# A decoder trunk on one core: the first FFN products formed as Strassen's seven block products, weights split in parts of 1024 columns

## Chip, core and metric

One core of a Trainium2 chip runs the whole program. The metric is device time in microseconds (us), the median of the runs. TensorE (PE) multiplies, VectorE (DVE), ScalarE (ACT) and GpSimd (POOL) work beside it, and SyncE (SP) starts the transfers. Instructions of one engine run in the order in which they stand; a tile scheduler fixes that order when the program is built, by priorities and by which buffers are free.

## What is computed

512 tokens of 1024 features pass through two layers. Each layer has a mixer and an FFN, both behind an RMS norm and added to the residual. The FFN is what changes most:

```python
def swiglu(x, w1, w3, w2):
    return (jax.nn.silu(x @ w1) * (x @ w3)) @ w2
```

`w1` and `w3` are 1024 x 2816, `w2` is 2816 x 1024. The mixer of layer 0 has six input projections to 512 columns, a linear recurrence and a retention; the one of layer 1 has five projections and attention in three branches.

## The kernel before

The residual `h` lies with features on the partitions, as 8 tiles of 128 x 512 tokens. Every float32 operand of a large product is split into a high part rounded to float32r and a low remainder, and the product is the sum of three passes, high-high, low-high and high-low (`mm3`, lines 123 to 125). For the normed residual `put_hg` does this (lines 136, 137); for weights `fetch` does it: a unit of 128 x 2048 is loaded into a buffer `wr` (pool of 2), and in four pieces of 512 columns ACT rounds `whi` (line 98) and DVE takes `wlo = wr - whi` (line 99; pools of 3 each). `unit` runs two units ahead of the products, at a priority a little above its place.

```python
 529  s = self.g2([P, S], name="s")
 530  V.tensor_tensor(s, pu, rb, op=ALU.mult)
 531  A.activation(s, s, AF.Silu)
 532  v = self.g2([P, S], name="v")
 533  V.tensor_tensor(v, pv, rb, op=ALU.mult)
 534  Q.tensor_tensor(v, v, s, op=ALU.mult)
 535  gh[j], gl[j] = ghq[:, j - q0, :], glq[:, j - q0, :]
 536  A.copy(gh[j], v)
 537  V.tensor_tensor(gl[j], v, gh[j].bitcast(F32), op=ALU.subtract)
```

An FFN (`ffn`, quoted from a hidden tile's end) works in two halves of 11 hidden tiles. For each hidden tile it forms two products, `ps_u` with w1 and `ps_v` with w3, each of 8 feature tiles times 3 passes = 24 matmuls with the weights stationary and 512 tokens moving. DVE scales both by the token's RMS factor (lines 530, 533), ACT applies silu (531), POOL multiplies (534), ACT and DVE split the result into `gh`, `gl` (536, 537). Then w2 is applied: 8 products `ps` of 11 x 3 matmuls, each added to `h` by DVE (552). In the second half of the last FFN the last two feature tiles run by halves of 256 tokens, and `final` scales and stores. While the residual is formed ACT squares each tile (148) and POOL sums the squares in `acc` (150); `stat_r` turns them into RMS factors after the first 24 matmuls of the FFN (matmul 160, DVE 163, POOL power 165).

A projection (`project` in layer 0, `proj` in layer 1) takes the tokens stationary: for each of 4 token tiles 8 x 3 matmuls into one PSUM bank `ps_t`, so that the first token tile already needs both units of the weights. PSUM has four banks in `psA`, two each in `psB` and `psC`. Transposes on PE (`ps_tr`) use `psC`.

Of the kernel before, what the change touches and what calls it, by code (L numbers as in the profile page):

```python
# [7 lines left out]

# [13 lines left out]
P = 128  # L22
# [19 lines left out]
QUADS = ((0, 4), (4, 4), (8, 3))  # L42


class Trunk:
    def __init__(self, ctx, tc, a, out, dbg=None, upto=99):
# [13 lines left out]
        self.units = []  # L60
        self.ready = []
# [24 lines left out]
    def plan(self, name, idx, n):  # L86
        self.units.append((self.a[name][idx], n))

    def blank(self):
        """buffers for the next unit: raw, its source, hi, lo"""  # L90
        src, n = self.units.pop(0)
        w = self.wr.tile([P, 2048], F32, tag="wr", name="wr")
        hi = self.wh.tile([P, 2048], F32R, tag="wh", name="whi")
        lo = self.wl.tile([P, 2048], F32R, tag="wl", name="wlo")
        return w[:, 0:n], src, hi, lo

    def split(self, w, hi, lo, c):
        self.nc.scalar.copy(hi[:, c], w[:, c])  # L98
        self.nc.vector.tensor_tensor(lo[:, c], w[:, c], hi[:, c].bitcast(F32), op=ALU.subtract)  # L99

    def fetch(self):
        with self.tc.high_priority(offset=10):
            w, src, hi, lo = self.blank()
            self.nc.sync.dma_start(w, src)
            n, k = w.shape[1], 4
            for i in range(k):
                self.split(w, hi, lo, slice(i * n // k, (i + 1) * n // k))
        self.ready.append((hi, lo))

    def prefetch(self, n):  # L110
        while self.units and len(self.ready) < n:
            self.fetch()

    def unit(self, ahead=2):
        self.prefetch(1 + ahead)
        return self.ready.pop(0)

    def mm3(self, ps, terms, first=True, last=True):
        """ps = sum over terms of (lhs_hi + lhs_lo)^T (rhs_hi + rhs_lo)"""
        mm = self.nc.tensor.matmul  # L120
# [12 lines left out]
    def put_hg(self, hg, k, h, gcol):  # L133
# [3 lines left out]
        nc.vector.scalar_tensor_tensor(lo, h, gcol, hi.bitcast(F32), op0=ALU.mult, op1=ALU.subtract)  # L137

# [14 lines left out]
    def stat_r(self, tiles=range(NT), last=None):  # L153
        """1/rms of token tiles as [P, len(tiles)]"""
# [13 lines left out]
    def stat_bc(self, r):  # L168
        """1/rms broadcast over partitions, [P, tokens] in PSUM"""
# [12 lines left out]
    def setup(self):  # L182
# [5 lines left out]
        # keeps the tensor engine busy until the first operands are there, so that its clock is up by then  # L188
# [5 lines left out]
        # loads the activation table  # L194
# [38 lines left out]
    def softplus(self):  # L233
        """4 and -8 times softplus(-lam), [P, 4]"""
# [27 lines left out]
    def layer0(self):  # L262
        nc, a = self.nc, self.a
        V, A, Q, T = nc.vector, nc.scalar, nc.gpsimd, nc.tensor
        for u in range(12):
            self.plan("w0t", u, 2048)
# [7 lines left out]
        wx = [self.blank() for _ in range(2)]  # L274
        self.stat_start()
        for k in range(KD):
            x = xin[k // 4][:, k % 4, :]
            w, src, hi, lo = wx[k // 4]
            c = slice((k % 4) * S, (k % 4 + 1) * S)
            nc.sync.dma_start(w[:, c], src[:, c])  # L280
# [43 lines left out]
        def units():  # L324
            return [tuple(x.rearrange("p (k c) -> p k c", k=4) for x in self.unit()) for _ in range(2)]
# [836 lines left out]
```

## Time and profile before

| | |
|---|---|
| median of 3 runs (1300.49 to 1301.39) | 1300.63 us |
| span of the profiled execution | 1299.8 us |
| PE busy (matmul) | 1272.5 us, 98%, 6067 instructions |
| PE weight loads | 1049.6 us, 81% |
| DVE busy | 708.7 us, 55% |
| ACT busy | 531.7 us, 41% |
| POOL busy | 300.0 us, 23% |
| granted TensorE clock, mean | 0.994 of full speed |

The profiled execution's own time is taken as its span and the 0.8 us that the median lies above it, 1300.6 us. The program runs through these stretches (us from the span's start): loads and layer 0's mixer to 231, its FFN 231 to 594, layer 1's mixer to 928, its FFN to 1292, the end of the stores. A busy PE does not mean a matmul at its peak: neighbouring matmuls overlap in the records, so the price of one is the distance between two starts.

### The profile page before, as it was taken

How to read it: one execution, taken by the hardware profiler on the slowest of the kernel's cores; microseconds unless marked ns; L12 is line 12 of the kernel's file. 1: busy time of each engine (PE TensorE's matmuls, PEld its weight loads, DVE VectorE, ACT ScalarE, POOL GpSimd, SP SyncE). 2: the span in 40 equal slices, each digit the busy share in tenths (PEclk: the TensorE clock that was granted, in tenths of full speed). 3: DMA queues.
4: the chain of work that ended last, by engine and by line, in shares of the span. 5: the costliest groups of instructions: out<-in, count | busy, mean ns of one | idle time of the engine just before them, and what ended most of it. 6: DMA issues, size and time to landing. Idle time of an engine off the chain costs nothing.

```text
span 1299.8 us, 15778 instructions
## 1 busy us (share of the span) xinstructions
PE 1272.5 (98%) x6067; PEld 1049.6 (81%) x6067; DVE 708.7 (55%) x1215; ACT 531.7 (41%) x1121; POOL 300.0 (23%) x304
## 2 busy tenths in 40 slices
PE   8979999999999999999999999999999999999997
PEld 6668888888888888888788877877888888888887
DVE  7994446555423554443345789987345443455433
ACT  6432253433222333334445578996333222233230
POOL 3351421211100111122000467672211100011111
PEclk9999999999999999999999999999999999999999
DMA  6213052222233222252110000024222223322221
GB/s 235 93 65 130 1 185 78 94 97 87 69 120 130 97 97 67 96 198 84 65 65 33 1 1 1 33 66 162 97 98 98 67 89 120 111 95 88 74 71 65
DMA packets 24042, 114.58 MB, mean 88 GB/s; under 512 B 2688, under 2 KB 5008, under 8 KB 14624
## 3 DMA queue, kind: packets, MB, share of 16 engines
q1 hardware_dynamic: 23776, 112.45, 24.9%
q8 instruction: 48, 0.79, 0.2%
q0 software_dynamic: 192, 1.13, 0.2%
q14 instruction: 26, 0.21, 0.0%
HBM read 109.38 MB, written 4.19 MB: 87 GB/s over the span
## 4 chain that ended last, share of the span: by engine, by line
PE 87%; DVE 7%; issue 2%; POOL 2%; ACT 1%; DMA 0%; POOLq 0%; SPq 0%; DVEq 0%; ACTq 0%
PE ps_v L123 6%; PE ps_u L125 6%; PE ps_v L125 6%; PE ps_u L123 6%; PE ps_u L124 6%; PE ps_v L124 6%; PE ps L125 6%; PE ps L123 6%; PE ps L124 6%; PE ps_t L123 4%; PE ps_t L124 4%; PE ps_t L125 4%; PE ps_tr L929 2%; PE ps_s L904 1%; PE ps_p L124 1%
## 5 line engine op out<-in xcount | busy, mean ns | idle before, releaser
L98 ACT CAST whi<-wr 128x512 fp32r<-128x512 f32 (+1 forms) x416 | 212.5, 576 | 394.2 <-PE ps_v L124 162.4
L99 DVE TENSOR_TENSOR wlo<-wr,whi 128x512 fp32r<-128x512 f32 (+1 forms) x416 | 294.4, 763 | 44.3 <-ACT whi L98 44.1
L534 POOL TENSOR_TENSOR v<-v,s 128x512 f32<-128x512 f32 x44 | 67.5, 1535 | 523.2 <-DVE v L533 506.9
L123 PE MATMUL ps<-gh,whi 128*128 128x512 f32 (+1 forms) x374 | 141.0, 377 | 0.0
L124 PE MATMUL ps<-gl,whi 128*128 128x512 f32 (+1 forms) x374 | 140.8, 376 | 0.0
L125 PE MATMUL ps<-gh,wlo 128*128 128x512 f32 (+1 forms) x374 | 140.8, 376 | 0.0
L533 DVE TENSOR_TENSOR v<-ps_v,rbc 128x512 f32<-128x512 f32 x44 | 30.4, 691 | 198.0 <-PE ps_v L125 198.0
L123 PE MATMUL ps_v<-hgh,whi 128*128 128x512 f32 x352 | 137.1, 390 | 0.0
L123 PE MATMUL ps_u<-hgh,whi 128*128 128x512 f32 x352 | 137.1, 390 | 0.0
L125 PE MATMUL ps_u<-hgh,wlo 128*128 128x512 f32 x352 | 137.0, 389 | 0.0
L124 PE MATMUL ps_u<-hgl,whi 128*128 128x512 f32 x352 | 136.9, 389 | 0.0
L124 PE MATMUL ps_v<-hgl,whi 128*128 128x512 f32 x352 | 136.9, 389 | 0.0
L125 PE MATMUL ps_v<-hgh,wlo 128*128 128x512 f32 x352 | 136.9, 389 | 0.0
L124 PE MATMUL ps_t<-wlo,hgh 128*128 128x512 f32 x288 | 113.3, 393 | 6.7 <-DVE wlo L99 6.7
L123 PE MATMUL ps_t<-whi,hgh 128*128 128x512 f32 x288 | 116.0, 403 | 0.0
L125 PE MATMUL ps_t<-whi,hgl 128*128 128x512 f32 x288 | 113.6, 394 | 0.0
L552 DVE TENSOR_TENSOR h<-ps,h 128x512 f32<-128x512 f32 x30 | 20.8, 692 | 135.4 <-PE ps L125 135.4
L924 POOL TENSOR_TENSOR prob<-prob,rs 128x384 f32<-128x384 f32 (+3 forms) x128 | 88.5, 726 | 1.9
L150 POOL TENSOR_TENSOR acc<-acc,sq 128x512 f32<-128x512 f32 (+1 forms) x35 | 48.9, 1398 | 172.1 <-ACT sq L148 171.9
L124 PEld LDWEIGHTS ps<-gl,whi 128*128 128x128 f32 x374 | 70.4, 188 | 13.0
L123 PEld LDWEIGHTS ps<-gh,whi 128*128 128x128 f32 x374 | 70.4, 188 | 12.8
L125 PEld LDWEIGHTS ps<-gh,wlo 128*128 128x128 f32 x374 | 70.4, 188 | 12.8
(282 smaller groups left out, 2291.7 us busy)
## 6 DMA issues: line engine op xcount, KB each, us to landing
wr<-wff SPq DMA_DIRECT2D x44, 1024.0 KB, 4.8
wr<-w SPq DMA_DIRECT2D x32, 704.0 KB, 4.0
wr<-w0t SPq DMA_DIRECT2D x10, 1024.0 KB, 4.8
wr<-w1t SPq DMA_DIRECT2D x10, 1024.0 KB, 4.9
wr<-w0o SPq DMA_DIRECT2D x4, 1024.0 KB, 4.8
wr<-w1o SPq DMA_DIRECT2D x4, 1024.0 KB, 4.9
wr<-w0t SPq DMA_DIRECT2D x8, 256.0 KB, 5.4
xin<-xT SPq DMA_DIRECT2D x8, 256.0 KB, 5.4
```

Of the source, the lines that this page charges most:

```text
L98: self.nc.scalar.copy(hi[:, c], w[:, c])
L99: self.nc.vector.tensor_tensor(lo[:, c], w[:, c], hi[:, c].bitcast(F32), op=ALU.subtract)
L123: mm(ps, ah, bh, start=(first and k == 0), stop=False)
L124: mm(ps, ah, bl, start=False, stop=False)
L125: mm(ps, al, bh, start=False, stop=(last and k == n - 1))
L150: nc.gpsimd.tensor_tensor(self.acc[:, c], self.acc[:, c], sq, op=ALU.add)
L533: V.tensor_tensor(v, pv, rb, op=ALU.mult)
L534: Q.tensor_tensor(v, v, s, op=ALU.mult)
L552: V.tensor_tensor(hm, ps, hm, op=ALU.add)
L904: T.matmul(u.ps, q, u.kh, start=True, stop=False)
L924: Q.tensor_tensor(x, x, u.rs[:, r, b:b + 1].broadcast_to([P, u.nk]), op=ALU.mult)
L929: T.transpose(u.pt[:, r * P:(r + 1) * P], u.p[:, r, b, j * P:(j + 1) * P], self.ident)
```

## The change

The hidden units of an FFN are now taken in three phases of two blocks: blocks of 512 units (`wff`), the last of 256 (`wfg`). For a block the product [v | u] = x [w3 | w1] is a product of 2 x 2 blocks: x by token halves of 256 and by even and odd feature tiles, the weights by even and odd feature tiles and by w3 and w1. `strassen` forms it from seven products, of two token tiles times four feature tiles times three passes = 24 matmuls each, with the tokens stationary and the weights' 512 columns moving. The combinations of x (`sg`: A11, A12, A22, S1 to S4) are formed once for a layer by `put_sg`; the combinations of the weights are formed on POOL in the raw buffers (line 160) before each part is split. The results are token-major; after silu and the multiplication (736) `turn` transposes them on PE (721) for w2, which is applied phase by phase.

Weights are split in parts of 1024 columns, ACT in two casts (136) and DVE in one subtraction (137). `whi` and `wlo` have 4 buffers of 1024 columns, `wr` 4 of 2048; the split runs three parts ahead. Projections go through `stream_t`: pairs of feature tiles outside, the four token tiles inside, in four banks at once. The attention's `probs` now takes its buffers from `wr` alone. The core of the diff:

```diff
-        self.wr = e(tc.tile_pool(name="wr", bufs=2))
-        self.wh = e(tc.tile_pool(name="wh", bufs=3))
-        self.wl = e(tc.tile_pool(name="wl", bufs=3))
+        self.wr = e(tc.tile_pool(name="wr", bufs=BUFS_W))
+        self.wh = e(tc.tile_pool(name="wh", bufs=BUFS_W))
+        self.wl = e(tc.tile_pool(name="wl", bufs=BUFS_W))
...
+    def split(self, x):
+        n = x.shape[1]
+        hi, lo = (t[:, 0:n] for t in self.pair())
+        k = 2 if n > 512 else 1
+        for i in range(k):
+            c = slice(i * n // k, (i + 1) * n // k)
+            self.nc.scalar.copy(hi[:, c], x[:, c])
+        self.nc.vector.tensor_tensor(lo, x, hi.bitcast(F32), op=ALU.subtract)
+        return hi, lo
...
+        def parts():
+            b11, b21 = self.take(), self.take()
+            h = [slice(c, min(c + 1024, n)) for c in range(0, n, 1024)]
+            sub = lambda o, x, y: Q.tensor_tensor(o, x, y, op=ALU.subtract)
+            b12 = None
+            for c in h:
+                yield self.split(b11[:, c])
+                b12 = self.take() if b12 is None else b12
+                sub(b11[:, c], b12[:, c], b11[:, c])
+            b22 = self.take()
+            for c in h:
+                yield self.split(b21[:, c])
+            for c in h:
+                sub(b12[:, c], b22[:, c], b12[:, c])
+            for c in h:
+                yield self.split(b11[:, c])
+                sub(b11[:, c], b22[:, c], b11[:, c])
+            for c in h:
+                yield self.split(b11[:, c])
+                sub(b21[:, c], b21[:, c], b11[:, c])
+            self.freed()
+            for x in (b22, b12, b21):
+                for c in h:
+                    yield self.split(x[:, c])
+                self.freed()
...
+    def put_sg(self, sg, k, h, gain):
+        V, A = self.nc.vector, self.nc.scalar
+        x = self.g2([P, 2, 256], name="xg")
+        A.activation(x.rearrange("p t s -> p (t s)"), h, AF.Copy, scale=gain[:, k:k + 1])
+        p = k // 2
+        def put(hi, lo, v):
+            A.copy(hi, v)
+            V.tensor_tensor(lo, v, hi.bitcast(F32), op=ALU.subtract)
+        if k % 2 == 0:
+            self.even = x
+            put(*(sg[0][:, z, p, :] for z in range(2)), x[:, 0])
+            return
+        x, y = self.even, x
+        put(*(sg[1][z][:, p] for z in range(2)), y)
+        u, v = (self.g2([P, 2, 256], name="sx") for _ in range(2))
+        V.tensor_tensor(u[:, 0], x[:, 1], y[:, 1], op=ALU.add)
+        V.tensor_tensor(u[:, 1], u[:, 0], x[:, 0], op=ALU.subtract)
+        V.tensor_tensor(v[:, 0], x[:, 0], x[:, 1], op=ALU.subtract)
+        V.tensor_tensor(v[:, 1], y[:, 0], u[:, 1], op=ALU.subtract)
+        for i, w in ((0, u), (2, v)):
+            put(*(sg[2][z][p // 2][:, p % 2, i:i + 2] for z in range(2)), w)
...
+        for j, (b, op) in enumerate((("X", "A11"), ("Y", "A12"), ("V", "S1"), ("X", "S2"), ("V", "S4"), ("X", "S3"), ("Z", "A22"))):
+            last(j)
...
+            for i in range(2):
...
+                self.mm3(o, [self.sg_at(sg, op, p, slice(i * P, (i + 1) * P)) + w.at((j * 4 + p) * n, (j * 4 + p + 1) * n) for p in range(4)], first, True, j in (3, 4, 5))
...
+                    u = vals.pop(t)
+                    Q.tensor_tensor(c, c, u, op=ALU.mult)
+                    later.append((6 if t < 2 else 8, partial(turn, t, c)))
+                def before(j):
+                    if j == 1 and self.rtok is None:
+                        self.rtok = self.stat_r()
+                    flush(j)
```

In `later` the number is the product before which the transposes stand: token tiles 0 and 1 before the seventh product of their own block, tiles 2 and 3 before the second product of the next block (8 minus 7 = 1), or in the middle of the w2 products after a phase's second block.

POOL at the change from a phase's first block to its second. Before, POOL had one multiplication for each hidden tile and nothing else between them:

```order
L534 TENSOR_TENSOR v_2013<-v_2013,s_2010 128x512
L534 TENSOR_TENSOR v_2083<-v_2083,s_2080 128x512
L534 TENSOR_TENSOR v_2155<-v_2155,s_2152 128x512
L534 TENSOR_TENSOR v_2225<-v_2225,s_2222 128x512
L534 TENSOR_TENSOR v_2295<-v_2295,s_2292 128x512
```

Of the change, second phase of layer 0's FFN (`part` are the halves of v and u, two multiplications for token tiles 0 and 1, then two for 2 and 3; `wr_2859`, `wr_2940`, `wr_2982` and `wr_2900` are the second block's raw weights B11, B12, B22 and B21):

```order
L736 TENSOR_TENSOR part_2919<-part_2919,part_2807 128x512
L736 TENSOR_TENSOR part_2933<-part_2933,part_2809 128x512
L160 TENSOR_TENSOR wr_2859<-wr_2940,wr_2859 128x1024
L160 TENSOR_TENSOR wr_2940<-wr_2982,wr_2940 128x1024
L160 TENSOR_TENSOR wr_2859<-wr_2940,wr_2859 128x1024
L160 TENSOR_TENSOR wr_2940<-wr_2982,wr_2940 128x1024
L736 TENSOR_TENSOR part_3001<-part_3001,part_2878 128x512
L736 TENSOR_TENSOR part_3017<-part_3017,part_2893 128x512
L160 TENSOR_TENSOR wr_2859<-wr_2982,wr_2859 128x1024
L160 TENSOR_TENSOR wr_2900<-wr_2900,wr_2859 128x1024
```

Four subtractions for the next block now stand between the multiplications of one block.

POOL at the end of layer 0's output projection, where the FFN's first weights are prepared. Before:

```order
L483 TENSOR_TENSOR tok_g<-tok_g,tok_q 128x512 x4
L150 TENSOR_TENSOR acc<-acc,sq 128x512 x7
L165 TENSOR_TENSOR rtok<-ms,mhalf 128x4
L534 TENSOR_TENSOR v<-v,s 128x512 x22
L150 TENSOR_TENSOR acc<-acc,sq 128x512 x3
```

Of the change (333 sums the squares, 348 is the power that gives the RMS factor):

```order
L663 TENSOR_TENSOR tok_g<-tok_g,tok_q 128x512 x4
L160 TENSOR_TENSOR wr<-wr 128x1024 x2
L333 TENSOR_TENSOR acc<-acc,sq 128x512 x4
L160 TENSOR_TENSOR wr<-wr 128x1024 x2
L333 TENSOR_TENSOR acc<-acc,sq 128x512 x3
L160 TENSOR_TENSOR wr<-wr 128x1024 x3
L348 TENSOR_TENSOR rtok<-ms,mhalf 128x4
```

The sums of squares now stand behind two subtractions and then two more, and the power behind another three.

DVE, same place, the last pair of feature tiles of the change (264 is the low part of a combination, 272 to 275 form it, 137 splits weights, 594 adds to `h`):

```order
L594 TENSOR_TENSOR h<-ps_f,h 128x512
L264 TENSOR_TENSOR sg<-xg,sg 128x256
L272 TENSOR_TENSOR sx<-xg 128x256
L274 TENSOR_TENSOR sx<-xg 128x256
L273 TENSOR_TENSOR sx<-sx,xg 128x256
L137 TENSOR_TENSOR wlo<-wr,whi 128x1024
L264 TENSOR_TENSOR sg<-xg,sg 128x512
L275 TENSOR_TENSOR sx<-xg,sx 128x256
L137 TENSOR_TENSOR wlo<-wr,whi 128x1024
L264 TENSOR_TENSOR sg<-sx,sg 128x512 x2
```

Before, each feature tile had one addition to `h` (414) and one low part (137) there, with splits of 512 columns in between.

## Rows read from the trace of the kernel before

**Rows 1.** The page: busy time with its share of the span, the chain by engine.

```profile
PE 1272.5 (98%) x6067; PEld 1049.6 (81%) x6067; DVE 708.7 (55%) x1215; ACT 531.7 (41%) x1121; POOL 300.0 (23%) x304
...
PE 87%; DVE 7%; issue 2%; POOL 2%; ACT 1%; DMA 0%; POOLq 0%; SPq 0%; DVEq 0%; ACTq 0%
```

**Rows 2.** Stretches: length, busy PE, PEld, DVE, ACT, POOL (instructions), granted clock, DMA.

```profile
210.00:232.00 22.00, 22.00 (x99) 18.22 (x98) 16.40 (x24) 13.18 (x24) 7.36 (x6) 1.00 0.29 96
232.00:360.00 128.00, 128.00 (x572) 106.03 (x571) 62.08 (x84) 39.37 (x73) 20.50 (x14) 1.00 0.25 86
```

**Rows 3.** Timeline of PE, FFN of layer 0 (start, duration, instruction, idle before and releaser).

```profile
231.42 0.39 PE L123 MATMUL ps_u<-hgh,whi 128*128 128x512 f32 x1
...
236.86 1.02 PE L160 MATMUL ps_stat<-ones,acc 128*128 128x1 f32 x8
```

**Rows 4.** Timeline of PE, the last FFN's tail by 256 tokens.

```profile
1273.04 0.28 PE L123 MATMUL ps<-gh,whi 128*128 128x256 f32 x1
...
1276.99 0.28 PE L123 MATMUL ps<-gh,whi 128*128 128x256 f32 x1
```

**Rows 5.** Timeline of PE, four transposes between matmuls in layer 1.

```profile
649.78 0.66 PE L749 MATMUL ps_tr<-ident,ks 128*128 128x128 f32 x4
650.19 0.48 PE L123 MATMUL ps_t<-whi,hgh 128*128 128x512 f32 x1
650.51 0.39 PE L124 MATMUL ps_t<-wlo,hgh 128*128 128x512 f32 x1
```

**Rows 6.** POOL's additions and multiplications by line: min/median/max ns, first and last start.

```profile
L534 POOL TENSOR_TENSOR v<-v,s x44: 1292/1580/1607, 246.6 to 1229.2; 128x512 f32<-128x512 f32 x44
...
L150 POOL TENSOR_TENSOR acc<-acc,sq x35: 740/1437/1862, 8.9 to 1287.1; 128x512 f32<-128x512 f32 x33, 128x256 f32<-128x256 f32 x2
```

**Rows 7.** Timeline of DVE, layer 0's projections, while POOL is idle.

```profile
66.45 0.75 DVE L350 TENSOR_TENSOR tok_q<-tok_q,b_qk 128x256 f32<-128x256 f32 x2
67.12 2.49 DVE L99 TENSOR_TENSOR wlo<-wr,whi 128x512 fp32r<-128x512 f32 x4
```

**Rows 8.** Timelines of DVE, POOL and ACT, one hidden tile of layer 0's FFN.

```profile
277.21 3.59 DVE L99 TENSOR_TENSOR wlo<-wr,whi 128x512 fp32r<-128x512 f32 x4
...
277.43 1.61 POOL L534 TENSOR_TENSOR v<-v,s 128x512 f32<-128x512 f32 x1 [9.27 <-DVE v L533]
...
276.42 2.18 ACT L98 CAST whi<-wr 128x512 fp32r<-128x512 f32 x4 [3.90 <-PE ps_v L124]
```

**Rows 9.** Timelines of POOL and DVE, layer 0's projections, both engines with work queued.

```profile
70.89 4.83 POOL L343 TENSOR_TENSOR tok_q<-e_qk,tab 128x512 f32<-128x512 f32 x1 [4.65 <-DVE e_qk L340]
75.67 5.85 POOL L371 TENSOR_TENSOR iv<-iv,e 128x512 f32<-128x512 f32 x4
...
75.75 2.92 DVE L350 TENSOR_TENSOR tok_q<-tok_q,b_qk 128x256 f32<-128x256 f32 x2 [1.19 <-POOL tok_q L343]
78.59 3.48 DVE L99 TENSOR_TENSOR wlo<-wr,whi 128x512 fp32r<-128x512 f32 x2
```

**Rows 10.** Timeline of PE at its longest wait, in layer 0's third projection.

```profile
97.05 0.79 PE L124 MATMUL ps_t<-wlo,hgh 128*128 128x512 f32 x1 [6.75 <-DVE wlo L99]
...
98.49 0.63 PE L124 MATMUL ps_t<-wlo,hgh 128*128 128x512 f32 x1
98.92 0.63 PE L125 MATMUL ps_t<-whi,hgl 128*128 128x512 f32 x1
```

**Rows 11.** Stretches around that wait, columns as in the second group.

```profile
93.00:94.00 1.00, 0.00 (x0) 0.00 (x0) 0.96 (x3) 0.00 (x0) 0.06 (x1) 0.76 0.00 0
...
99.00:100.00 1.00, 1.00 (x4) 0.81 (x3) 1.00 (x3) 0.00 (x0) 0.52 (x1) 0.50 0.67 106
100.00:101.00 1.00, 1.00 (x5) 0.77 (x5) 1.00 (x4) 0.00 (x0) 1.00 (x1) 0.82 0.54 156
```

**Rows 12.** The page: DMA issues, KB and median us to landing; DVE's additions from PSUM.

```profile
L533 DVE TENSOR_TENSOR v<-ps_v,rbc 128x512 f32<-128x512 f32 x44 | 30.4, 691 | 198.0 <-PE ps_v L125 198.0
...
wr<-wff SPq DMA_DIRECT2D x44, 1024.0 KB, 4.8
```

More of the change, by code (lines that the diff above doesn't have):

```diff
@@ L101, in fetch, with raw @@
-    def fetch(self):
-        with self.tc.high_priority(offset=10):
-            w, src, hi, lo = self.blank()
-            self.nc.sync.dma_start(w, src)
[L105 to L108, printed above, removed]
-    def prefetch(self, n):
[L111 to L115, printed above, removed]
+    def raw(self):
+        return self.wr.tile([P, 2048], F32, tag="wr", name="wr")
@@ new lines, in pair, with load, freed, take @@
+    def pair(self):
+        return tuple(p.tile([P, 1024], F32R, tag=t, name=n) for p, t, n in ((self.wh, "wh", "whi"), (self.wl, "wl", "wlo")))
+    def load(self):
+        while self.sources and self.n_loaded < self.n_freed + BUFS_W:
+            src, n = self.sources.pop(0)
+            w = self.raw()[:, 0:n]
+            self.nc.sync.dma_start(w, src)
+            self.loaded.append(w)
+            self.n_loaded += 1
+    def freed(self):
+        self.n_freed += 1
+        self.load()
+    def take(self):
+        self.load()
+        return self.loaded.pop(0)
@@ new lines, in split, with plan @@
+    def split(self, x):
[7 more added lines that the diff above has]
+        return hi, lo
+    def plan(self, name, idx, n, part=1024):
+        self.sources.append((self.a[name][idx], n))
+        def parts():
+            w = self.take()
+            for c in range(0, n, part):
+                yield self.split(w[:, c:c + part])
+            self.freed()
+        self.streams.append(parts())
@@ L116, in unit, with next_part @@
+    def prefetch(self, n):
+        while self.streams and len(self.ready) < n:
+            with self.tc.high_priority(offset=10):
+                x = next(self.streams[0], None)
+            if x is None:
+                self.streams.pop(0)
+            else:
+                self.ready.append(x)
+    def next_part(self):
+        self.prefetch(1 + self.ahead)
         return self.ready.pop(0)
-    def mm3(self, ps, terms, first=True, last=True):
-        mm = self.nc.tensor.matmul
+    def unit(self, part=1024):
+        return Weights(self, part)
@@ L121, in mm3 @@
+    def mm3(self, ps, terms, first=True, last=True, onto=False):
+        mm = partial(self.nc.tensor.matmul, skip_group_check=onto)
         n = len(terms)
@@ L273, in layer0 @@
         xin = [self.b8([P, 4, S], name="xin") for _ in range(2)]
-        wx = [self.blank() for _ in range(2)]
+        raws = [self.raw() for _ in range(2)]
+        wx = [self.pair() for _ in range(4)]
         self.stat_start()
@@ L672, in layer1, with flush @@
         deferred = []
-        def flush():
-            while deferred:
-                deferred.pop(0)()
-        for t in range(NT):
-            ps = proj(t, w) if t else ahead
-            flush()
+        now = 0
+        def flush(lag=3):
+            nonlocal now
+            now += 1
+            while deferred and deferred[0][0] <= now - lag:
+                deferred.pop(0)[1]()
+        for t, ps in first:
+            if ps is None:
+                flush()
+                continue
             kvs = []
```

357 lines of the change are left out of this document (233 added, 124 removed).

## Prediction

> **What bounds the kernel now.** I read the page first: PE is busy for 98% of the span and holds 87% of the chain that ended last [rows 1]. In an FFN stretch PE never rests, while DVE has 62, ACT 39 and POOL 21 of 128 us [rows 2]. So less PE work shortens the program directly, as long as the weights arrive in time. The price of a matmul is the distance of starts: 24 matmuls of 512 columns take 236.86 - 231.42 = 5.44 us, 0.2267 each [rows 3]; 33 of 256 columns take 3.95 us, 0.12 each [rows 4]; four transposes take 0.41 us and make the next matmul 0.09 late, 0.50 a group [rows 5].
>
> **The change, PE's work.** By the order of both programs there are 402 fewer matmuls of 512 columns and 276 more of 256: -402 x 0.2267 = -91.1 us and +276 x 0.12 = +33.1 us (the blocks of 256 units use short matmuls, so they save little). The token-major results need 40 groups of four transposes (20.0 us) and 8 of two (some 0.30 each, 2.4 us); two groups that spread the RMS factor go (-1.0). PE's work: **-36.6 us**, give or take 2. Only waits of PE can take this back, and each does so in full, since nothing on PE is slack.
>
> **What the other engines must now do.** A full block is seven products of 5.44 us and 16 transposes, 38.1 + 2.0 = 40.1 us of PE. In it DVE splits 14 parts of 1024 columns. Two-input operations from SBUF take 0.34 us for 256 columns and 0.60 for 512 when POOL is idle [rows 7], so 1.13 for 1024 by the same slope: 15.8 us. POOL subtracts 8 pieces of 1024 and multiplies 4 of 512; two-input work takes 0.74 for 256 and 1.29 for 512 at the least [rows 6], so 2.39 for 1024: 24.3 us. ACT's 28 casts (2.18 us for four [rows 8]) are 15 us; with 8 scalings, 4 silus and 4 copies 24, which fits. One load takes 4.8 us to land [rows 12], hidden by four raw buffers.
>
> Each sum alone is below 40.1. But DVE and POOL get in each other's way. Four splits take 2.41 us with POOL idle and 3.51 when one multiplication of POOL falls among them [rows 7, 8]: one of the four waits out nearly the whole of it. Where both have work queued, four instructions of POOL take 5.85 us, and four of DVE that alone take 1.9 take 6.4 [rows 9]. The Trainium skill, SBUF — State Buffer, section Who interferes with whom, says this outright: a DVE instruction with two SBUF inputs and a GpSimd instruction that reads SBUF hold the shared port pair one at a time, the second blocks until the first is done. By that rule the trace agrees, and the rule speaks against this change; without it the sum below would end near 1272. Serialised, the block needs 15.8 + 24.3 = 40.1 us of that port, exactly PE's time, so every dependency between the two engines becomes a wait.
>
> **The waits, one place at a time** (times from a block's start; a PE result is taken as ready 0.2 us after the next matmul starts).
>
> *Second product of a phase's second block.* POOL has four subtractions for the second block queued ahead of the multiplications for token tiles 2 and 3 of the first. The first subtraction overwrites a part once it is split, which needs a buffer freed 18 matmuls into the sixth product: 27.2 + 4.1 + 0.2 = 31.5, plus ACT 1.1 and DVE 1.13, 33.8. Then 4 x 2.39 + 2 x 1.29 = 12.2, 46.0; four splits of DVE want the port in between (4.5), 50.5, and the last transposes end at 51.0. PE arrives at 44.6 and could be through at 45.6. The wait is 0.9 with no interference and 5.5 with all of it; I take 5.0, since DVE always has a split queued there. With the block of 256 units the first product is only 2.9 us long, but two subtractions fewer stand in the way: 1 to 4, I take 3.8. Four of the first kind and two of the second: **+27.6** (6 to 30).
>
> *Fourth product of a phase's first block.* Its weights, B22 - (B12 - B11), are formed in the buffer of B12 - B11, so after that is split: buffer free at 4.3, split by 6.6, subtraction 9.0, a subtraction for the seventh product 11.4 + 1.13 for a split in between, second piece 16.1, ACT 17.3. POOL is by then in its next subtraction until 18.6, DVE ends at 19.7; PE wants it at 17.9. Wait 1.8, none without interference. Five places (the sixth is in the next paragraph): **+9** (0 to 12).
>
> *Start of layer 0's FFN.* The second half of the output projection is 8 x 12 matmuls, 21.8 us. DVE now has 8 additions from PSUM of 0.69 [rows 12], for each pair of feature tiles five operations of 256 and three of 512 columns from SBUF (3.5 us), and four splits: 24 us, where it had 16.4 in 22 [rows 2]. POOL has four subtractions and seven sums, 18.6 us. From the first split, 14.9 us before the first product, to the low part of tile 6 that this product needs for its last rows there are 17.5 us of DVE and 17.3 of POOL. One after the other, with 1.5 us overlapped, they end 18.4 us after the product could start; it needs them at 2.0. Without interference some 3 us remain, because ACT has 40 casts and scalings there, 22 us. DVE can also hold the port over several instructions, as when one of POOL's took 4.83 us [rows 9]; then it would be about 9. I take **+16** (3 to 20), as the additions to h stand behind operations that need the port. The sums of squares and the power behind the subtractions come on top, some 3 us, inside the upper end.
>
> *Start of layer 1's FFN.* There the projection has 24 matmuls for each tile, 43.5 us, and the same work fits; late are the last sums: **+2.5** (0 to 6).
>
> *Clock.* After PE had been idle for 6.75 us the granted clock was 0.50, the 1.2 GHz level; matmuls stood 0.43 us apart for some 3.2 us, which cost 1.5 us [rows 10, 11]. It had fallen about 3 us into the wait. Five waits of 4 us or more may do the same, I take 1 us each: **+5** (0 to 9).
>
> *Projections by parts.* The wait of 6.75 us came because a first token tile needs all the weights at once. Now a quarter is enough, but PSUM's four banks must be emptied by the same busy DVE before the next projection starts, and that stretch's DVE work is unchanged: **-4** (0 to -8).
>
> W2's 43.5 us a phase split a part each 5.44 us with no subtraction beside them late in it: nothing. The attention's buffers stay four deep: nothing, as PE waits there for little now. The tail has fewer short matmuls before the factor is needed, under 1 us either way: nothing.
>
> **Sum** against this execution's own 1300.6 us (the median is 1300.63): -36.6 + 27.6 + 9 + 16 + 2.5 + 5 - 4 = +19.5, so **1320 us**. All low ends give -32, 1268; all high ends +45, 1346.
>
> **Rivals.**
> *DVE and POOL hardly disturb each other* (faster). If POOL's instructions slip into DVE's pauses, as in most hidden tiles now, the six changes of block cost 6, layer 0's start 3 to 5, the rest nothing: -36.6 - 4 + 6 + 5 + 1 = -29, **1272**. For it: DVE's own 15.8 us leave 24 us free in each block. Against: rows 8 and 9. What decides is the total of the waits: under 40 us the change gains. Chance 0.26.
> *Half of it* (faster). Changes of block 3 us each (18), the start 8, the fourth products 4: -36.6 - 4 + 30 = -11, **1290**. For it: DVE held the port over eight instructions in rows 9, and with splits done early POOL's order matters less. Chance 0.10.
> *The port becomes the bound* (slower still). If each alternation also costs a latency of 0.3 us, the 26 instructions of a block need 8 us more than PE, 48 instead of 40; over the ten full blocks, less what the w2 stretches absorb, some 45 us in place of the 37 above, with the upper ends at the starts and of the clock: -36.6 - 4 + 45 + 20 + 6 + 9 = +39, **1340**. For it: the six instructions of rows 9 leave no pause unused. Against: POOL has nothing to do in the w2 stretches, and can run ahead there. Chance 0.10.
> *Gain and waits cancel*, within 2.6 us of now: a coincidence of sums, chance 0.05.
>
> **How the numbers follow.** Within 0.2% is 2.6 us, about what measurements of this kernel can tell from no change. The forecast keeps 0.49. Faster: 0.26 + 0.10 = 0.36; same 0.05; slower 0.49 + 0.10 = 0.59. The range runs from the first rival to just short of the third, 1270 to 1338, and leaves about 0.1 outside at either end; the forecast's own range, with its sizes uncertain, is 1304 to 1336.
>
> **What would show it.** Right: transposes `ps_tr` (721) waiting for POOL `part` (736), some 5 us, at six places; POOL's subtractions (160) and DVE's splits (137) well over 2.4 and 1.13 us each; a wait of PE of more than 10 us at the first product of layer 0's FFN; PE's busy time without waits some 37 us lower. Wrong: those waits under 2 us, splits near 1.13 us with POOL busy, then it is the first rival; or PE waiting for splits in every product, then the third.

## The result: 1349.13 us, 3.7% slower, and the profile after

| | before | after |
|---|---|---|
| median | 1300.56 us (4 runs, 1300.32 to 1301.39) | 1349.13 us (4 runs, 1347.54 to 1351.59) |
| span of the profiled execution | 1299.8 us | 1347.4 us |
| granted TensorE clock, mean | 0.994 | 0.972 |

The ratio is 1.0373, 95% interval 1.0358 to 1.0388. The sign was as forecast; the change costs 48.6 us where +19.5 was predicted, and 1349 lies above the range (1270 to 1338).

The page of the changed kernel: busy times, the chain that ended last, and three groups (busy us, mean ns of one | idle before, releaser):

```profile
PE 1265.2 (94%) x6109; PEld 1037.9 (77%) x6109; DVE 874.6 (65%) x1131; ACT 674.6 (50%) x1351; POOL 543.6 (40%) x396
...
PE 64%; POOL 13%; DVE 10%; issue 6%; ACT 5%; DMA 1%; POOLq 0%; DVEq 0%; SPq 0%; ACTq 0%
...
L137 DVE TENSOR_TENSOR wlo<-wr,whi 128x1024 fp32r<-128x1024 f32 (+1 forms) x256 | 392.8, 1540 | 226.0 <-ACT whi L136 214.5
...
L160 POOL TENSOR_TENSOR wr<-wr 128x1024 f32<-128x1024 f32 x88 | 241.2, 2748 | 203.1 <-DVE wlo L137 197.3
L736 POOL TENSOR_TENSOR part<-part 128x512 f32<-128x512 f32 (+1 forms) x48 | 71.4, 1492 | 197.7 <-ACT part L730 155.9
```

PE held 87% of the chain before [rows 1] and holds 64% now, POOL has 13 and DVE 10. No engine but PE is busy for more than two thirds of the span, so none of them is full: they wait for each other. A split takes 1.54 us on the mean (1.55 for those of 1024 columns alone), a subtraction 2.75.

Where the time went, by stage (layer 0's mixer, its FFN, layer 1's mixer, its FFN; us, then busy us and instructions of each engine, granted clock, DMA). The kernel before:

```profile
0.00:231.42 231.42, 217.54 (x1041) 177.72 (x1041) 155.51 (x259) 97.01 (x164) 77.22 (x54) 0.98 0.33 115
231.42:591.92 360.50, 360.50 (x1597) 298.57 (x1596) 165.87 (x246) 112.10 (x215) 47.79 (x32) 1.00 0.30 105
591.92:927.59 335.67, 330.56 (x1750) 269.00 (x1749) 225.10 (x462) 216.98 (x540) 128.70 (x186) 1.00 0.15 52
927.59:1299.76 372.17, 363.89 (x1683) 304.31 (x1681) 162.21 (x249) 105.64 (x202) 46.27 (x33) 0.99 0.26 88
```

The same stretches of the changed kernel:

```profile
0.00:234.48 234.48, 220.31 (x1041) 178.40 (x1041) 154.91 (x228) 96.16 (x163) 76.88 (x53) 0.97 0.31 113
234.48:615.84 381.36, 353.90 (x1633) 292.55 (x1632) 247.38 (x230) 182.74 (x330) 170.21 (x79) 0.96 0.29 102
615.84:960.59 344.75, 333.79 (x1750) 269.05 (x1749) 239.88 (x448) 221.53 (x547) 136.08 (x189) 1.00 0.14 47
960.59:1347.41 386.82, 357.17 (x1689) 297.90 (x1687) 232.47 (x229) 174.20 (x313) 160.41 (x77) 0.96 0.24 85
```

+3.1, +20.9, +9.1 and +14.7 us. In the FFNs POOL's busy time has more than tripled and DVE's grown by half; the granted clock fell from 1.00 and 0.99 to 0.96. Layer 1's mixer, in which the weights' buffers, the projections' order and, at its end, the sums of x changed, gives 9 us that the prediction had at nothing.

The waits of PE in the changed kernel (total us, times, longest):

```profile
PE ps_tr L721 <- POOL part L736: 23.3, 9, 4.1
PE ps_X L205 <- ACT sg L263: 10.1, 3, 5.9
PE ps_X L206 <- DVE wlo L137: 9.2, 7, 2.1
PE ps_t L205 <- DVE e_qk L523: 4.1, 2, 2.9
PE ps_t L206 <- DVE wlo L137: 3.2, 1, 3.2
PE ps_X L207 <- DVE sg L264: 3.0, 3, 2.6
PE ps_g L876 <- DVE hgl L239: 2.9, 1, 2.9
```

All waits sum to 74.5 us, where the kernel before had 20.5. The first row is the changes of block, the second, third and sixth are the starts of the FFNs and the fourth products: they are where the prediction put them. The wait at layer 0's start is shorter than the 10 us named as a sign: 10.2 us in five pieces, the longest 5.9. One change of block in full, layer 0's second phase (second block from 423.8 us). POOL (start us, us, what, how many):

```profile
424.59 6.68 POOL L160 TENSOR_TENSOR wr<-wr 128x1024 f32<-128x1024 f32 x2
431.23 3.46 POOL L736 TENSOR_TENSOR part<-part 128x512 f32<-128x512 f32 x2
434.66 2.36 POOL L160 TENSOR_TENSOR wr<-wr 128x1024 f32<-128x1024 f32 x1
```

DVE beside it:

```profile
417.52 1.23 DVE L137 TENSOR_TENSOR wlo<-wr,whi 128x1024 fp32r<-128x1024 f32 x1 [1.10 <-ACT whi L136]
...
419.65 2.71 DVE L137 TENSOR_TENSOR wlo<-wr,whi 128x1024 fp32r<-128x1024 f32 x1 [0.25 <-ACT whi L136]
422.28 1.28 DVE L725 TENSOR_TENSOR gl<-ps_tr,gh 128x512 fp32r<-128x512 f32 x2
...
426.30 2.76 DVE L137 TENSOR_TENSOR wlo<-wr,whi 128x1024 fp32r<-128x1024 f32 x1
429.36 2.99 DVE L137 TENSOR_TENSOR wlo<-wr,whi 128x1024 fp32r<-128x1024 f32 x1 [0.31 <-ACT whi L136]
```

And PE:

```profile
433.52 2.34 PE L721 MATMUL ps_tr<-ident,part 128*128 128x128 f32 x8 [4.12 <-POOL part L736]
```

A split takes 1.23 us while POOL is idle and 2.7 to 3.0 beside its subtractions; the last two subtractions before the multiplications take 6.68 us, 3.34 each, where one alone takes some 2.4 (line 160's median is 2.41). DVE's instructions with one input in PSUM are not stretched: the two of line 725 at 422.28 us take 1.28 us while POOL subtracts, and the 20 of them that lie wholly within a subtraction take 0.67 to 0.69 us each, as with POOL idle (median 0.68). PE has stood since 429.4; the first of the two multiplications lets it go on at 433.5, the second ends at 434.7.

Then the clock. These are the stretches of the two FFNs with the clock at 0.50, the 1.2 GHz level (columns as above); the kernel before has none in its FFNs up to its tail:

```profile
241.30:254.80 13.50, 7.42 (x16) 4.68 (x17) 13.50 (x19) 8.80 (x16) 5.14 (x3) 0.50 0.00 1
302.70:306.00 3.30, 2.86 (x9) 2.47 (x10) 2.77 (x2) 2.19 (x4) 3.22 (x3) 0.50 0.00 0
432.40:439.20 6.80, 5.57 (x17) 4.41 (x18) 3.41 (x3) 2.28 (x4) 6.72 (x4) 0.50 0.00 0
...
988.80:992.10 3.30, 3.30 (x9) 2.57 (x8) 1.44 (x2) 0.73 (x2) 0.00 (x0) 0.50 0.91 315
...
1282.40:1285.70 3.30, 3.30 (x18) 3.30 (x17) 3.30 (x3) 0.83 (x2) 0.84 (x1) 0.50 0.14 22
sum 50.20, PE 39.36 PEld 30.96 DVE 38.05 ACT 26.97 POOL 31.54; mean PE 4.37 PEld 3.44 DVE 4.23 ACT 3.00 POOL 3.50
```

Nine stretches with 39.4 us of PE's work in them, which at the upper level takes half: 19.7 us lost. Each begins within a wait or at most 1.4 us after one. The one from 988.8 us follows a wait of 2.14 us, the last one a wait of 2.87, so the fall did not need the 4 us that the prediction asked for.

### The profile page after: what moved, and what is told of

Its sections match the earlier page's. It is cut to its first block, busy times and chain, and to the rows that moved or that the text cites. A ratio compares the mean times of both kernels' runs of the same rounds, so it can differ in the third digit from the quotient of the medians.

```text
span 1347.4 us, 16429 instructions
## 1 busy us (share of the span) xinstructions
PE 1265.2 (94%) x6109; PEld 1037.9 (77%) x6109; DVE 874.6 (65%) x1131; ACT 674.6 (50%) x1351; POOL 543.6 (40%) x396
## 4 chain that ended last, share of the span: by engine, by line
PE 64%; POOL 13%; DVE 10%; issue 6%; ACT 5%; DMA 1%; POOLq 0%; DVEq 0%; SPq 0%; ACTq 0%
POOL wr L160 10%; PE ps L206 5%; PE ps L205 5%; PE ps L207 5%; PE ps_t L205 4%; PE ps_t L207 4%; PE ps_t L206 4%; DVE wlo L137 3%; PE ps_X L207 3%; PE ps_X L206 3%; PE ps_X L205 2%; PE ps_tr L1170 2%; PE ps_V L207 2%; PE ps_V L206 2%; PE ps_V L205 2%
## 5 line engine op out<-in xcount | busy, mean ns | idle before, releaser
L137 DVE TENSOR_TENSOR wlo<-wr,whi 128x1024 fp32r<-128x1024 f32 (+1 forms) x256 | 392.8, 1540 | 226.0 <-ACT whi L136 214.5
L136 ACT CAST whi<-wr 128x512 fp32r<-128x512 f32 (+1 forms) x512 | 290.9, 615 | 406.6 <-PE ps L206 120.8
L160 POOL TENSOR_TENSOR wr<-wr 128x1024 f32<-128x1024 f32 x88 | 241.2, 2748 | 203.1 <-DVE wlo L137 197.3
L736 POOL TENSOR_TENSOR part<-part 128x512 f32<-128x512 f32 (+1 forms) x48 | 71.4, 1492 | 197.7 <-ACT part L730 155.9
L205 PE MATMUL ps_X<-whi,sg 128*128 128x512 f32 (+1 forms) x288 | 110.5, 384 | 11.3 <-ACT sg L263 10.1
L206 PE MATMUL ps_X<-wlo,sg 128*128 128x512 f32 (+1 forms) x288 | 110.7, 384 | 9.2 <-DVE wlo L137 9.2
L207 PE MATMUL ps_X<-whi,sg 128*128 128x512 f32 (+1 forms) x288 | 110.4, 383 | 3.0 <-DVE sg L264 3.0
L760 DVE TENSOR_TENSOR h<-ps,h 128x512 f32<-128x512 f32 x46 | 31.8, 691 | 74.3 <-PE ps L207 74.3
L1155 ACT ACTIVATE prob<-ps_s,nm 128x384 f32<-128x384 f32 (+3 forms) x128 | 68.1, 540 | 15.7 <-DVE nm L1151 14.7
L205 PEld LDWEIGHTS ps_X<-whi,sg 128*128 128x128 f32 x288 | 56.0, 194 | 23.5 <-ACT sg L263 11.7
L206 PEld LDWEIGHTS ps_X<-wlo,sg 128*128 128x128 f32 x288 | 55.9, 194 | 21.5 <-DVE wlo L137 12.0
```

The lines of the kernel that those rows point to most:

```text
L136: self.nc.scalar.copy(hi[:, c], x[:, c])
L137: self.nc.vector.tensor_tensor(lo, x, hi.bitcast(F32), op=ALU.subtract)
L160: sub = lambda o, x, y: Q.tensor_tensor(o, x, y, op=ALU.subtract)
L205: mm(ps, ah, bh, start=(first and k == 0), stop=False)
L206: mm(ps, ah, bl, start=False, stop=False)
L207: mm(ps, al, bh, start=False, stop=(last and k == n - 1))
```

## Experiments

The theory after reading this (POOL, later PORT): the FFN's waits come from POOL's and DVE's instructions excluding each other, and the half clock comes from the waits. Its rivals: DVE and ACT are simply loaded (LOAD), POOL's own occupancy is enough (QUEUE), the half clock comes from the form of the products (CLOCK).

**Transposes moved to a later product.**

```diff
-                    later.append((6 if t < 2 else 8, partial(turn, t, c)))
+                    later.append((6 if t < 2 else 10, partial(turn, t, c)))
```

> Only the place of the transposes of token tiles 2 and 3 of a phase's first block moves: before the fourth product of the second block instead of before its second. Theory POOL (the multiplications stand behind four subtractions on POOL and DVE's splits take the port in between): the multiplications still end some 11 us into the second block, PE wants them after 16.3 us, so the waits for part at the six block changes vanish (22.8 us of gaps in the changed kernel) and with them the half clock behind them (some 14 us more, the block changes are 37 us longer than their matmuls): about 1312 us. Rival LOAD (DVE and ACT are full in a block and only show it at the transposes): the wait reappears at the next split that is late, in the third or fourth product, and the time stays over 1335 us. Rival CLOCK (the half clock comes from the form of the products, not from waits): the gaps go, the half clock stays, about 1327 us.

Measured 1345.62 us, ratio 1.034 (1.0322 to 1.0358): 3.5 us won instead of 37. The waits for `part` fell from 23.3 to 4.1 us, but those for splits rose from 9.2 to 20.5; all waits of PE sum to 72.6 us, where they were 74.5. PE in the second block of layer 0's second phase, fourth product:

```profile
441.47 0.50 PE L206 MATMUL ps_X<-wlo,sg 128*128 128x512 f32 x1 [0.34 <-DVE wlo L137]
444.35 0.50 PE L205 MATMUL ps_X<-whi,sg 128*128 128x512 f32 x1 [1.45 <-ACT whi L136]
447.21 0.80 PE L206 MATMUL ps_X<-wlo,sg 128*128 128x512 f32 x1 [2.36 <-DVE wlo L137]
```

The wait moved 11 us on, to the parts formed by POOL's later subtractions; the half clock followed it. So the wait at the change of block is only where the lateness of POOL and DVE first shows. My expectation fell, in the form that LOAD gave; whether load or port, the next runs tell.

**The subtractions left out.**

```diff
-            sub = lambda o, x, y: Q.tensor_tensor(o, x, y, op=ALU.subtract)
+            sub = lambda o, x, y: None
```

> The 88 subtractions of weight blocks on POOL are left out; the buffers' raw blocks are split in their place, so the products multiply the wrong blocks and the work of PE, ACT and DVE is that of the changed kernel. Theory POOL: the waits at the block changes (37 us with their clock) and before the fourth products (14 us) vanish, and part of the 16 and 7 us at the two layer starts: 1349 - 37 - 14 - 8 = about 1290 us. DVE's splits fall to 1.2 us each in the FFNs but for those beside multiplications. Rival LOAD: waits move to other places, over 1325 us. If it stays above 1300.6 even so, subtractions alone don't explain why the changed kernel is slower than the one before.

Measured 1285.6 us, ratio 0.9881 (0.9866 to 0.9896). The subtractions cost 63.5 us, and without them the seven products do gain. LOAD falls: matmuls, casts and splits were all there.

**The subtractions on DVE.**

```diff
-        Q = self.nc.gpsimd
+        Q = self.nc.vector
```

(in `plan_set`)

> The 88 subtractions run on DVE instead of POOL, each right behind the split that frees its buffer. Theory POOL: DVE has 8 x 1.13 = 9 us more to do in a block of 40 (25 us in all with the splits, where POOL and DVE needed the port for 40), POOL keeps only multiplications and sums of squares, so the waits at the block changes fall under 1 us and those before the fourth products under 2; the start of layer 0's FFN, where DVE is the later one, gets no better: 1349 - 37 - 10 = about 1302 us. Rival LOAD (DVE is the scarce engine, 875 us busy): its 100 us more make PE wait for splits in most products, over 1349 us.

Measured 1309.69 us, ratio 1.006 (1.0044 to 1.0077): 39 us won by giving the busier engine 88 instructions more. It is 8 us above the expectation, mainly because the multiplications still wait:

```profile
PE ps_tr L721 <- POOL part L736: 13.3, 14, 1.5
PE ps_stat L343 <- POOL acc L333: 6.8, 1, 6.8
PE ps_X L206 <- DVE wlo L137: 4.2, 1, 4.2
```

Fourteen waits of about 1 us for POOL's multiplications, and 6.8 us at layer 0's start for POOL's sums of squares.

**The wait filled with matmuls.** In `turn`, for t = 2 of a first block in phases 0 and 1:

```diff
+                    if first and t == 2:
...
+                        for _ in range(18):
+                            T.matmul(pt, x, y, start=True, stop=True)
```

> At four block changes (phases 0 and 1 of both layers) 18 matmuls of 512 columns, whose result is overwritten, stand before the late transposes: 4.1 us of work in a wait of 4.1 us. Theory CLOCK BY WAITS: the transposes start no later than before, and the granted clock stays at its upper level over the next product; the 72 extra matmuls cost nothing and the clock's share of these changes (some 2 us each, 8 in all) comes back: about 1341 us, with half-clock time 10 to 16 us lower in these stretches. Rival CLOCK: it falls anyway, 1349 us or more. If PE's work were what bounds these places, 4 x 4.1 = 16 us more: 1365 us.

Measured 1353.37 us, ratio 1.0393 (1.0376 to 1.0409): not the 8 us faster that were expected. The median is 4 us above the changed kernel's, but the two intervals overlap (1.0358 to 1.0388 there), so a loss is not shown either. At the first change the clock stayed up, at the second it fell later and for half as long (in the changed kernel 0.50 over 3.3 and 6.8 us there):

```profile
302.00:306.50 4.50, 3.70 (x18) 3.13 (x19) 1.53 (x3) 0.59 (x1) 4.42 (x3) 1.00 0.00 0
432.40:439.20 6.80, 5.25 (x19) 4.13 (x18) 1.96 (x4) 1.18 (x2) 6.72 (x4) 0.75 0.01 2
```

But the scheduler, with other times in its plan, put one more split ahead of the late multiplication: at the second change it ended 11.9 us after the block's start instead of 10.9, and PE waited 1.55 us even so. All waits of PE fell from 74.5 to 63.8 us, so some 11 of the 16.3 us of added matmuls did lie in waits, and half-clock time at these four places fell from 20.5 to 10.2 us; that the clock's share comes back in time was not shown.

**Streamed projections in the kernel before.**

```diff
+            banks = [self.psA("ps_t") for _ in range(NT)]
+            for i, t in ((i, t) for i in range(4) for t in range(NT)):
...
-                self.mm3(ps, [... for k in range(KD)])
+                self.mm3(ps, [... for k in (2 * i, 2 * i + 1)], i == 0, i == 3)
```

(the LRU's steps, and the priority of the products that empty the banks of q and k, as in the changed kernel)

> The kernel before with one part of the change alone: layer 0's projections go by pairs of feature tiles over four banks, the LRU's steps placed as in the changed kernel; buffers, splits and FFN stay as they were. Theory STREAM (four token tiles now end within one quarter of a projection, so DVE must empty four banks at once, beside the LRU's scans): the wait of 6.75 us for the low part goes, waits for the emptied banks come in its place as in the changed kernel (2.9 and 1.2 us there), and layer 0's mixer takes 0 to 4 us more than the kernel before: 1301 to 1305 us. Rival BUFFERS (the changed kernel's mixer is late because of its parts of 1024 columns in four buffers): the wait goes and nothing takes its place, as the prediction had it: about 1296 us.

Measured 1303.14 us, ratio 1.002 (1.001 to 1.0029), inside what STREAM gave. The wait for a low part is gone, and in its place stands

```profile
PE ps_t L123 <- DVE e_qk L345: 7.0, 2, 6.2
```

one wait of 6.2 us for a bank that DVE must empty. The projections' -4 of the prediction is wrong in its sign, and not for the smaller buffers. Whether the order of the products or the place of the LRU's steps makes this wait, the run does not tell apart; the candidate below does.

**pew later, first try.** The line `pes = [pe_weights(x) for x in range(2)]` in `layer1` moved behind `r = self.stat_r()`.

> In the changed kernel, POOL's two multiplications of 1024 columns for the compressed keys' weights (pew) are issued after the RMS factors of layer 1's mixer instead of before its gates. Theory PORT: in the changed kernel they run from 612.9 to 617.6 us and stretch a split of DVE to 2.90 us and the low part of the residual to 2.39 us, so PE waits 2.9 us for the last hgl and loses 1.6 us more to the half clock; without them there the wait falls under 0.5 us: 1349 - 4 = about 1345 us. Rival SHORT TILES (w2's last tiles now come each 4.1 us instead of 7.5 us, and DVE and ACT are late whatever POOL does): the wait stays over 2 us, 1349 us.

Measured 1347.09 us, ratio 1.0352 (1.0336 to 1.0369), 2 us below the changed kernel, within the spread of either. Not conclusive: POOL ran pew at 611.3 us, between the same sums of squares as before. With nothing else to do there the scheduler kept its place.

**Multiplications on DVE as well.** Upon the run with the subtractions on DVE:

```diff
-                    Q.tensor_tensor(c, c, u, op=ALU.mult)
+                    V.tensor_tensor(c, c, u, op=ALU.mult)
```

> The subtractions of weight blocks (as with the subtractions on DVE before) and the multiplications after silu run on DVE; POOL keeps only the sums of squares in an FFN. Theory PORT: with the subtractions on DVE alone there were 14 waits for part of 13 us in all, as each multiplication waited for the port between DVE's instructions and held DVE up in turn; on DVE a multiplication is one more instruction of some 0.7 us and no one waits for the port: 1309.7 - 13 - 1 for the clock = about 1296 us. Rival LOAD: DVE then has 16 + 9 + 6 + 3 + 3 = 37 us in a block of 40 and falls behind: 1310 us or more.

Measured 1294.96 us, ratio 0.9954 (0.9941 to 0.9968). As expected to 1 us: the changed kernel's work with POOL taken out of it is faster than before, with DVE doing all of it. LOAD falls again.

**A candidate.** On top of that, in `put_sg` the sums for the last two pairs of feature tiles are collected and formed after the loop, pew moves as above and the LRU steps at `t % 4 == 1`.

```diff
+        if defer is not None and p >= 2:
+            defer.append(sums)
+        else:
+            sums()
```

> A candidate that undoes what the runs have shown to cost: subtractions and multiplications on DVE, the sums of x for the last four feature tiles of layer 0's FFN formed after its first operands, pew later, the LRU's steps spread over two projections. Expected by theory PORT: 1296 for the first two, 8 us less at the start of layer 0's FFN (15 us of waits and clock there with the subtractions on DVE), 4 at the start of layer 1's mixer, 2 in layer 0's projections: about 1282 us. By rival LOAD over 1300 us.

Measured 1284.54 us, ratio 0.9877 (0.9864 to 0.9891), where 1282 was expected. Layer 0's FFN went from 359.7 us in the run before to 352.1, nearly the 8 expected. The move of pew gave nothing: the wait for the last `hgl` is still there with 2.7 us. With the LRU's steps half as often, layer 0's projections take 151.4 us from their first matmul to their last; the run before took 153.5, the changed kernel 153.6, the kernel before 151.2 and the kernel before with streamed projections 154.1. So the streamed order by itself costs next to nothing; the 2 to 3 us come with the LRU's steps so close together. PE's waits in that stretch are no fewer (7.4 us in five waits for a bank, 7.3 in three waits in the changed kernel), but none is over 1.9 us and the clock stays up.

**pew later, in earnest.** The line moved as in the first try, and in `pe_weights`, with `self.power` the power of the RMS factors:

```diff
-            Q.tensor_tensor(t, cw[:, x], ..., op=ALU.mult)
+            self.after(Q.tensor_tensor(t, cw[:, x], ..., op=ALU.mult), self.power)
```

> In the run with pew later, POOL still took pew between two sums of squares, since it had nothing else to do: the edit did not move it. Here pew is ordered behind POOL's power for the RMS factors of layer 1's mixer. Theory PORT: with POOL doing only sums of squares beside the last tiles of w2, DVE's splits and low parts there take 1.2 and 0.75 us, the last hgl comes in time, and the 2.9 us wait and its half clock go: about 1345 us. Rival SHORT TILES: the wait stays over 1.5 us, 1348 us.

Measured 1345.22 us, ratio 1.0337 (1.0322 to 1.0352). The wait for the last `hgl` is gone and layer 1's mixer takes 341.7 us instead of 344.8: PORT, 3 of the 9 us there.

**POOL writes and reads nothing.**

```diff
-            sub = lambda o, x, y: Q.tensor_tensor(o, x, y, op=ALU.subtract)
+            sub = lambda o, x, y: [Q.memset(o, 0.5) for _ in range(2)]
```

> Each subtraction of weight blocks on POOL is replaced by two fills of the same 1024 columns with a constant: POOL writes the same buffer at the same place in its queue, but reads nothing, so the products multiply other numbers. Theory PORT (POOL and DVE exclude each other when DVE has two inputs in SBUF and POOL reads SBUF): beside the fills DVE's splits take 1.2 us, as with POOL idle, and only those beside multiplications and sums of squares are longer; if two fills take about the 2.4 us of a subtraction, the six changes of block keep no more than 1 us of wait each and the time is about 1290 to 1300 us. Rival QUEUE (POOL's own work delays the multiplications, whatever it reads): with fills of 2.4 us the waits at the block changes stay over 3 us and the time over 1325 us. If splits beside the fills take over 2 us, writes exclude DVE too.

Measured 1285.65 us, ratio 0.9876 (0.9862 to 0.989). A fill takes 0.96 us, two 1.91, so the queue was shorter as well; hence the next run.

**The same, as long as a subtraction.**

```diff
+            sub = lambda o, x, y: [Q.memset(z, 0.5) for z in (o, o, o[:, 0:512])]
```

> The last run's two fills took 1.91 us where a subtraction takes 2.39, so POOL's queue was a fifth shorter too. Here each subtraction is replaced by two fills of 1024 columns and one of 512, 5 x 0.48 = 2.39 us: POOL is busy as long as with subtractions and reads nothing; the products multiply other numbers. Multiplications can start between the three fills, up to 1.4 us earlier than between subtractions. Theory PORT: DVE's splits keep some 1.25 us, the chain of four pieces and two multiplications takes 9.6 + 2.6 = 12.2 us without a wait for the port in it (15.9 in the changed kernel), the waits at the block changes are 1 to 2 us each where they were 4.1 and more, about 1293 us. Rival QUEUE (POOL's occupancy alone makes the waits): waits over 3 us at the block changes and at the fourth products, over 1325 us.

Measured 1286.55 us, ratio 0.9887 (0.9871 to 0.9904), 63 us below the changed kernel. The groups of DVE's splits and of POOL's two fills, and PE's wait for the multiplications:

```profile
L137 DVE TENSOR_TENSOR wlo<-wr,whi 128x1024 fp32r<-128x1024 f32 x248 | 312.3, 1263 | 234.9 <-ACT whi L136 224.6 <-POOL wr L160 4.1 <-issue 2.4
...
L160 POOL MEMSET wr<- 128x1024 f32 x176 | 166.3, 956 | 186.4 <-DVE wlo L137 94.9 <-DMA wr<-wff 51.9 <-DVE h L760 29.0
...
L160 POOL MEMSET wr<- 128x512 f32 x88 | 46.1, 527 | 2.9
```

```profile
PE ps_tr L721 <- POOL part L736: 3.8, 5, 1.3
```

Three fills take 2 x 0.956 + 0.527 = 2.44 us, no less than a subtraction alone, in the same queue before the same splits. DVE's split keeps 1.26 us, where it took 1.55 in the changed kernel, and the waits for `part` fall from 23.3 to 3.8 us. The splits that run beside nothing but these pieces show it without a mean over other work: 46 beside fills take 1.22 us on the mean, at most 1.23, just as with POOL idle; in the changed kernel 51 beside subtractions take 2.52, at most 3.42. A fill also need not wait for the second block that a subtraction reads, but POOL's subtractions had waited only 2.8 us for loads in all. QUEUE falls: what costs is that POOL reads SBUF while DVE has two inputs there, not that POOL is busy. The Trainium skill, SBUF — State Buffer, section Who interferes with whom, says that a DVE instruction with two SBUF inputs contends with a GpSimd instruction that reads SBUF, and not with one that only writes it; these two runs agree.

**The candidate with pew in its place.**

> The candidate with pew ordered behind the power in layer 1's mixer, where its edit had not moved it. Theory PORT: the wait for the last hgl (2.7 us there) and 1 us of half clock go: 1284.5 - 3.5 = 1281 us. Rival SHORT TILES: 1284 us.

Measured 1281.99 us, ratio 0.9848 (0.9834 to 0.9862): the fastest of the runs that leave nothing out, 1.5% under the kernel before and 5% under the changed one. Its two FFNs, in the profiled execution of 1286.04 us (columns as above):

```profile
232.13:585.85 353.72, 346.27 (x1633) 289.20 (x1632) 262.01 (x292) 180.60 (x326) 19.47 (x12) 0.99 0.31 110
...
928.95:1284.26 355.31, 345.52 (x1689) 291.46 (x1687) 248.39 (x288) 171.03 (x307) 14.78 (x12) 0.99 0.27 92
```

POOL is nearly idle, DVE is busy for 0.7 of the time and PE never waits more than 2.4 us for it there: 353.7 and 355.3 us where the kernel before took 360.5 and 372.2.

## Why the prediction was right in sign and wrong in size

The span grew by 47.6 us. The waits of PE account for 74.5 - 20.5 = +54.0 and the half clock for some +23: 19.7 in the FFNs, and half of PE's 9.5 us in two stretches of the mixers, 4.8, where the stretch of before [rows 11] held 3.3 us of matmuls and cost 1.7. The rest, PE's work and its restarts after the waits, is 47.6 - 54.0 - 23 = -29. The rows below the first are waits alone, but for the clock's; 2 us of other waits, most of them at the program's end, have no row.

| term | predicted | measured |
|---|---|---|
| PE's work | -36.6 | -29, restarts included |
| changes of block | +27.6 | +22.8 (4.7, 4.1, 2.9, 4.1, 4.1, 2.9) |
| fourth products | +9 | +10.1 (2.1, 1.5, 1.5, 2.1, 1.5, 1.5) |
| start of layer 0's FFN | +16 | +10.2 |
| start of layer 1's FFN | +2.5 | +3.1 |
| clock | +5 | +23 |
| projections streamed | -4 | +0.3 |
| layer 1's mixer | no term | +5.6 |

**What held.** That PE's work falls by nearly 36.6: in the three runs without POOL's subtractions, whose FFNs take 348 to 357 us with some 5 us of waits in each instead of 360 and 372, the same account (span, less PE's waits, less half of its work at the lower level) gives -33 to -35. It gives -29 in the changed kernel, which has 26 waits more than the kernel before; that their restarts take the difference is an inference. The places of the waits and their sizes: 46 us in the FFNs where I had put 55, at the very matmuls named. The cause behind them, the shared access of DVE and POOL to SBUF: the runs with writes alone, and DVE's unstretched instructions with an input in PSUM, show it apart from POOL's occupancy. The first rival, no interference and 1272 us, is what the runs without POOL's reads come near to (1285 to 1287, with the mixers' 10 us still in them).

**The step that failed: "Clock. ... Five waits of 4 us or more may do the same, I take 1 us each: +5 (0 to 9)."** It counted too few falls and priced them too low. Nine stretches of the FFNs fell to the lower level, and they cost 2.2 us each on the mean, 3.7 at layer 0's start, by the count of half of PE's work in them (no run shows this price by itself); the prediction's own row gave 1.5, and it took 1 without a reason. I took the one fall in [rows 10, 11] as what a wait needs; here waits of 2.1 to 2.9 us were followed by a fall too, five of them in the FFNs, while four of 1.5 us at fourth products were not. The trace of the kernel before already spoke against that condition, in a fall near the program's start that I had not read: after a wait of 1.86 us the clock was at 0.50 as well (the wait, then the stretch with columns as above).

```profile
21.40 0.50 PE L296 MATMUL ps_x<-hgl,whi 128*128 128x512 f32 x1 [1.86 <-DVE hgl L137]
22.00:25.00 3.00, 3.00 (x8) 2.34 (x7) 2.86 (x10) 0.00 (x0) 0.00 (x0) 0.50 0.02 5
```

And a wait is dearer than its length: at 429.4 us, 4.1 us of waiting were followed by 5.7 us at half speed, which cost 2.8 more. With the clock at its measured size the sum would have been 1338, the edge of the range. Beyond that, PE's work gave 7.6 us less than forecast, the projections and layer 1's mixer cost 4.3 and 5.6 more, and the four kinds of places in the FFNs 9 less.

**Two smaller steps that failed.** "Projections by parts ... -4": I named the condition myself (four banks to be emptied by the busy DVE) and then did not price it; with the LRU's steps where the change puts them, the streamed order costs the kernel before 2.5 us, one wait of 6.2 us for a bank in place of the 6.75 for a low part. "The attention's buffers stay four deep: nothing": layer 1's mixer lost 9.1 us, some 3 for the last `hgl` (the run with pew behind the power took these back), 2.4 for a low part of the output projection that comes late, and smaller waits in the attention. The last two are read from the trace and were not tried. The ends of the sum are also added wrongly: the stated low ends give -36 and the high ends +40, not -32 and +45; the range was drawn from the rivals and does not rest on them.

**What the third rival had.** Its number (1340) was nearest and its words half right: moving the transposes alone won 3.5 us, so POOL and DVE were late throughout, not at one place in the queue. Its mechanism, 0.3 us for each alternation, was not needed: the four subtractions from 418.9 us took 12.4 us with DVE's splits between them, less than four of 2.4 and three of 1.2.

## What to carry to other kernels

Before giving elementwise work to an engine that looks idle, ask whether it reads SBUF while DVE has two inputs there: 88 subtractions that DVE does in 1.2 us each cost 39 us more on POOL, the engine with 60% of its time free. Price a wait of PE with the clock behind it: in the changed kernel the clock was at its lower level after every wait over 2 us but one, and the nine stretches in the FFNs were worth some 2 us each. And a wait that disappears when one instruction is moved shows its cause only if the time goes with it.

## What was not expected of the hardware

POOL's fills of 1024 float32 columns take 0.956 us, those of 512 take 0.527, and leave DVE's two-input work untouched (1.22 us a split, as alone), where subtractions of the same total length stretch it to 2.52 us on the mean and as much as 3.42. DVE's work with one input in PSUM is untouched by the subtractions too (0.68 us within one, 0.68 alone). The granted clock fell after waits of only 1.86 and 2.14 us and stayed at its lower level for 3.3 us of unbroken matmuls; the same length of wait can also pass without a fall (2.36 us before layer 1's output projection in the changed kernel, but followed by half clock in the first candidate; 1.86 us near the start, with a fall in both kernels and none in the kernel before with streamed projections).
